# A two-layer decoder trunk on one core: the scheduler orders all queues by its detailed timeline

## The chip, the core and the metric

One core of a Trainium2 chip. The metric is the device time of one execution in microseconds, taken from several runs. The core's engines are TensorE (PE, matrix products), VectorE (DVE), ScalarE (ACT), GpSimd (POOL) and SyncE (SP, which here issues all DMAs). Each has its own queue and works through it in order; semaphores tie the queues together.

## The reference

Two layers over x of 512 tokens by 1024. Each layer normalises and modulates x by a condition vector c, projects it to 3,740 columns, runs four kinds of attention on them (A dilated, B native sparse, C gated linear, D sliding window with sinks), multiplies each by its own gate, projects back, normalises again and adds the result, gated, to x:

```python
shift, scale, gate = jnp.split(jax.nn.silu(c) @ w_ada + b_ada, 3, axis=-1)
h = rms_norm(x, ln_pre) * (1.0 + scale[:, None]) + shift[:, None]
u = split_columns(h @ w_in)
o_a = dilated_attention(a_q, a_k, a_v)
o_b = nsa_attention(b_q, b_kc, b_vc, b_ks, b_vs, b_kw, b_vw, b_g)   # compresses keys and values by w1, w2
o_c = rms_norm(gla_attention(c_q, c_k, c_v, log_a), gla_norm)
o_d = banded_attention(d_q, d_k, d_v, SWA_WIN - 1, sinks)
mixed = jnp.concatenate([o_a * silu(a_z), o_b * silu(b_z), o_c * silu(c_z), o_d * silu(d_z)], axis=-1)
return x + gate[:, None] * rms_norm(mixed @ w_out, ln_post)
```

## The kernel before

All data is float32. Every large product is made of three matmuls on split operands: the operand is cast to a rounded high part (`HH`, `whi`) and the rest is kept as a low part (`HL`, `wlo`); PE adds high·high, high·low and low·high. ACT makes `whi` (L475) and DVE `wlo` (L478).

*Tiles.* x is four row tiles of 128 tokens, `x0` to `x3`. Its normalised, transposed form lies in `HH`/`HL`. Names below carry a serial number (tp_3763), which is that of the tile in the program.

*Start.* `startup` loads x, norms it, transposes (L703), modulates and splits it (`HL` at L711). The modulation is computed by DVE: one L290 reduces a 128x512 slice `wmod` of the modulation weights; 32 of these belong to each layer.

*Projection.* `proj` produces columns transposed (`mm_T`, tile `mmT`, L525, 24 matmuls) or by row tile (`mm_TM`, tile `mmTM`, L536). `load_piece` (L487) loads raw weights into a ring of four buffers, `wraw`; `split_w` puts their halves into a ring of three.

*Attention.* In a layer C comes first (`attn_c`), then B, A and D. C forms the log decay `la` in two DVE steps (L836, L837), sums it on PE (`bp`, L841), gathers the values `vs` by small DMAs (L824) and ends with value products (L953). B multiplies two compression matrices w1, which take slots of the raw-weight ring (`hid`, L1052), transposes the result (`hT`, L1061), and goes on to compressed keys (`kcp`) and scores. In B, A and D a unit is: scores `sc` (L638, L639), maximum `m` (DVE, L755), exponential `p` (ACT, L757), reciprocal and scaling (DVE, L763 to L768), transposes `pT` (L771), copies, value products (L785).

*Beside it.* `merge` calls the attention generators and, between their steps, the projection (`proj`), the first part of the output projection (`out1`, tile `yo`, L1169) and `extras`: in layer 0 the 32 L290 of layer 1, and in both layers the gate, for which DVE sums 16 slices `wada` into `aac` (L348 the first of eight, L350 the rest: "macs" below), PE adds over partitions (L377), DVE adds a row `adab` (L378) and POOL multiplies by `adal` (L380). All slices `wmod`, `wada`, `adab`, `adal` share one ring of two buffers.

*Between the layers.* For each row tile `out2` adds the last part of the output projection (`yo2`, L1169, L1216), then on DVE `y` (L1224), `yg` (L1232) and `xr` (L1237), and norms `y` for the next layer (L438). `turn` transposes it on PE (`tp`, L454, eight matmuls), modulates half by DVE and half by ACT (`hf`, L464, L462), casts `HH` (ACT, L467) and subtracts `HL` (DVE, L468). `mm_TM` then projects the tile's C columns (`mmTM`, 24 matmuls of 332 columns). The program writes these in the order out2 of tile 0, turn 0, out2 of tile 1, turn 1, and so on, then the four products.

*What sets the order.* The source gives each instruction a priority by the place where it is written, shifted here and there by constants. The tile framework's scheduler then simulates the engines in time, takes at each moment for each engine the ready instruction of best priority, and so fixes every queue: PE, DVE, ACT, POOL and SP's DMA issues. Nothing is reordered at run time. The constant `TLS` (line 21) chooses which of two models of time this simulation uses; it is handed over in `make`.

Of the kernel before, what the change touches and what calls it, by code (L numbers as in the profile page):

```python
# [17 lines left out]
EPS = 1e-6  # L18
BIG = 1e30
PRE = 2  # L20
TLS = False
B = dict(raw=4, w=3, mx=3, v4=5, dv=2, ad=2, qk=16, g=8, p=3, sz=4, pt=3, sm=4)
QT = QH = QL = QG = 0
QX = 60
# [1325 lines left out]
def make(arrays):  # L1350
# [3 lines left out]
    out = nc.dram_tensor('out_y', (S, D), F32, kind="ExternalOutput").ap()  # L1354
    with tile.TileContext(nc, schedule_with_timeline_sim=TLS) as tc:
        build(tc, A, out)
# [9 lines left out]
```

## Time and profile before

| | us |
|---|---|
| runs | 694.17, 694.81, 696.92 |
| median | 694.81 |
| the profiled execution | 697.9 |
| its span | 695.7 |

| engine | busy us | share of the span |
|---|---|---|
| PE | 649.8 | 93% |
| PE weight loads | 524.5 | 75% |
| DVE | 498.6 | 72% |
| ACT | 336.8 | 48% |
| POOL | 31.1 | 4% |

The mean granted clock of PE is 0.986 of full speed. HBM moved 125 GB/s over the span. Rows of matmuls are pipelined, and their ends are modelled: a matmul's recorded time is longer than the distance from its start to that of the next. In a table by stretch, length minus busy time of PE is the time in which it did nothing at all. The stretches of the program in the profiled execution are: start 0–52, C of layer 0 52–124, projections and the compression of B 124–174, B, A and D of layer 0 174–313, end of the first output projection 313–348, passage to layer 1 348–384, projections 384–410, C 410–462, projections and compression 462–506, B, A and D 506–657, end of the output 657–696.

### The profile page before, as it was taken

The page shows a single profiled execution, that of the slowest core. Times are in us where ns is not written, and L with a number is a line of the kernel's source. Part 1 is how long each engine was busy: PE and PEld are TensorE (multiplying, and loading weights), DVE is VectorE, ACT ScalarE, POOL GpSimd, SP SyncE. Part 2 cuts the span into 40 slices and gives each one's busy share as a digit, 9 for nine tenths or more (in the row PEclk, how much of TensorE's full clock was granted, in tenths as well). Part 3 has the DMA queues.
Part 4 walks back from the last instruction along what each step waited for, and adds up shares of the span by engine and source line. Part 5 has one row for each costly group of instructions (what it writes and reads, how often), then busy time and mean ns, then how long its engine had stood idle before and what let it go on. Part 6 is the DMA issues. An engine that isn't in the chain of part 4 may idle for free.

```text
span 695.7 us, 11980 instructions
## 1 busy us (share of the span) xinstructions
PE 649.8 (93%) x4460; PEld 524.5 (75%) x4460; DVE 498.6 (72%) x1291; ACT 336.8 (48%) x748; POOL 31.1 (4%) x57
## 2 busy tenths in 40 slices
PE   3999889989998999999998989899999999999996
PEld 1797766877777767779996768678777777778895
DVE  5985889666868787784598467743588878768656
ACT  5454444155565555663475244425545436435432
POOL 2000000000001100000012000000000000000000
PEclk9999999999999999999999999999999999999999
DMA  8955764657204444112642681212520021111143
GB/s 299 391 218 166 256 195 138 185 180 272 77 1 138 136 110 133 34 32 81 207 169 79 180 262 43 63 61 91 165 78 32 17 75 32 46 46 46 48 155 116
DMA packets 38163, 87.89 MB, mean 126 GB/s; under 512 B 4185, under 2 KB 7769, under 8 KB 38106
## 3 DMA queue, kind: packets, MB, share of 16 engines
q1 hardware_dynamic: 38106, 87.14, 38.7%
q8 instruction: 35, 0.57, 0.3%
q14 instruction: 22, 0.18, 0.1%
HBM read 81.88 MB, written 5.24 MB: 125 GB/s over the span
## 4 chain that ended last, share of the span: by engine, by line
PE 58%; DVE 17%; DMA 12%; ACT 6%; issue 4%; POOL 1%; SPq 1%; DVEq 0%; POOLq 0%; ACTq 0%
PE mmT L525 19%; PE yo L1169 9%; PE mmTM L536 5%; PE pT L771 5%; DMA wmod<-in_w_mod 4%; PE ob L785 3%; DMA vs<-vd 3%; DVE wlo L478 2%; DMA wraw<-in_w_in 2%; PE a L719 2%; PE yo L1216 2%; PE sc L638 2%; DVE wmod L290 2%; PE od L1007 2%; PE oa L785 2%
## 5 line engine op out<-in xcount | busy, mean ns | idle before, releaser
L525 PE MATMUL mmT<-HH,whi 128*128 128x512 f32 (+1 forms) x352 | 142.8, 406 | 1.4 <-ACT whi L475 1.4
L525 PE MATMUL mmT<-HH,wlo 128*128 128x512 f32 (+1 forms) x352 | 142.6, 405 | 0.4 <-DVE wlo L478 0.4
L525 PE MATMUL mmT<-HL,whi 128*128 128x512 f32 (+1 forms) x352 | 142.3, 404 | 0.0
L757 ACT ACTIVATE p<-p,m 128x256 f32<-128x256 f32 (+3 forms) x128 | 68.8, 538 | 66.9 <-DVE m L755 62.5
L478 DVE TENSOR_TENSOR wlo<-wraw,whi 128x1024 fp32r<-128x1024 f32 (+3 forms) x60 | 72.2, 1205 | 33.2 <-ACT whi L475 32.9
L475 ACT CAST whi<-wraw 128x1024 fp32r<-128x1024 f32 (+3 forms) x60 | 61.5, 1027 | 56.1 <-PE mmT L525 36.8
L525 PEld LDWEIGHTS mmT<-HH,wlo 128*128 128x128 f32 (+1 forms) x352 | 66.2, 188 | 16.1 <-issue 1.5
L525 PEld LDWEIGHTS mmT<-HH,whi 128*128 128x128 f32 (+1 forms) x352 | 66.4, 189 | 15.3 <-ACT whi L475 1.8
L525 PEld LDWEIGHTS mmT<-HL,whi 128*128 128x128 f32 (+1 forms) x352 | 66.4, 189 | 14.0 <-issue 1.2
L771 PE MATMUL pT<-cst,p 128*128 128x128 f32 x296 | 48.9, 279 | 6.0 <-DVE p L768 2.2
L536 PE MATMUL mmTM<-whi,HH 128*128 128x256 f32 (+1 forms) x160 | 48.6, 304 | 3.2 <-ACT HH L467 2.4
L755 DVE CUSTOM_DVE_ANT_0 p<-sc,cst 128x128 f32<-128x128 f32 (+3 forms) x96 | 44.8, 482 | 7.7 <-PE sc L639 7.3
L771 PEld LDWEIGHTS pT<-cst,p 128*128 128x128 f32 x296 | 33.3, 140 | 22.5 <-issue 11.8
L536 PE MATMUL mmTM<-whi,HL 128*128 128x256 f32 (+1 forms) x160 | 47.4, 297 | 0.4 <-DVE HL L468 0.4
L536 PE MATMUL mmTM<-wlo,HH 128*128 128x256 f32 (+1 forms) x160 | 47.2, 295 | 0.0
L1169 PE MATMUL yo<-wlo,HH 128*128 128x256 f32 x144 | 41.9, 291 | 0.0
L1169 PE MATMUL yo<-whi,HH 128*128 128x256 f32 x144 | 41.7, 290 | 0.0
L1169 PE MATMUL yo<-whi,HL 128*128 128x256 f32 x144 | 41.1, 286 | 0.0
L536 PEld LDWEIGHTS mmTM<-whi,HH 128*128 128x128 f32 x160 | 31.0, 194 | 6.1 <-ACT HH L467 3.5
L638 PE MATMUL sc<-k,x 128*128 128x128 f32 (+3 forms) x96 | 32.7, 352 | 0.5 <-DVE m L755 0.2
L778 DVE COPY pt<-pT 128x256 f32<-128x256 f32 (+3 forms) x60 | 28.4, 498 | 6.4 <-PE pT L771 5.5
L536 PEld LDWEIGHTS mmTM<-whi,HL 128*128 128x128 f32 x160 | 30.9, 194 | 1.9 <-DVE HL L468 0.9
(273 smaller groups left out, 1342.2 us busy)
## 6 DMA issues: line engine op xcount, KB each, us to landing
wraw<-in_w_in SPq DMA_DIRECT2D x52, 512.0 KB, 4.1
wmod<-in_w_mod SPq DMA_DIRECT2D x64, 256.0 KB, 5.4
wada<-in_w_gate SPq DMA_DIRECT2D x32, 256.0 KB, 3.1
wor<-in_w_out SPq DMA_DIRECT2D x12, 512.0 KB, 3.3
w<-in_w SPq DMA_DIRECT2D x8, 512.0 KB, 4.7
vs<-vd SPq DMA_DIRECT2D x24, 128.0 KB, 9.8
x<-in_x SPq DMA_DIRECT2D x8, 256.0 KB, 5.2
wor<-in_w_out SPq DMA_DIRECT2D x8, 256.0 KB, 2.9
```

What stands on the lines that cost most here:

```text
L290: DVE.tensor_tensor_reduce(wt, wt, csr[:, 512 * h:512 * h + 512], 0.5, init, ALU.mult, ALU.add, dst)
L475: ACT.copy(hi, raw)
L478: eng.tensor_tensor(out=lo, in0=raw, in1=hi, op=ALU.subtract)
L525: PE.matmul(acc[:m], a, b, start=(n == 0), stop=(n == 23))
L536: PE.matmul(acc[:, :ncol], a, b, start=(n == 0), stop=(n == 23))
L638: PE.matmul(out, q[e][:, qs], k[e][0][:, ks], start=True, stop=False)
L755: DVE.tensor_tensor_reduce(p[:, c], sc[:, c], mask, -0.125, 1e38 if sink is None else sink[0][:, es[j]:es[j] + 1], ALU.add, ALU.min, m[:, ...
L757: ACT.activation(p[:, c], p[:, c], AF.Exp, bias=m[:, j:j + 1], scale=-1.0, accum_out=lsum[:, j:j + 1])
L771: PE.transpose(tp[:, b:b + 128], p[:, b:b + 128], C('ident'))
L778: DVE.tensor_copy(dst, src)
L785: PE.matmul(o[hs, q0:q1], vt[:, kb, vc:vc + 64], PT[:, 512 * kb:512 * kb + q1 - q0], start=(first and kb == 0), stop=(last and kb == 3), s ...
L1169: PE.matmul(acc[:, :n_], a, b, start=(n == 0), stop=(n == last))
```

## The change

The scheduler's simulation of time uses its detailed timeline in place of its plain one. The source of the computation is untouched: the same instructions, tiles, buffers and priorities, but every queue's order is drawn up anew.

```diff
-TLS = False
+TLS = True
```

Three places, each shown from the queue before and from the queue after.

VectorE between the first modulated piece of row tile 1 and its `HL`, at the passage between the layers; before:

```order
L464 TENSOR_SCALAR hf32_3768<-tp_3763,adags_624,adass_623 128x128
L464 TENSOR_SCALAR hf32_3780<-tp_3775,adags_624,adass_623 128x128
L1232 TENSOR_TENSOR yg_3835<-y2_3181,gl_2188 128x512
L464 TENSOR_SCALAR hf32_3768<-tp_3763,adags_624,adass_623 128x128
L1237 SCALAR_TENSOR_TENSOR xr_3789<-yg_3835,rstd_3839,xr_3789 128x512
L478 TENSOR_TENSOR wlo_3597<-wraw_3594,whi_3596 128x996
L478 TENSOR_TENSOR wlo_3603<-wraw_3600,whi_3602 128x664
L468 TENSOR_TENSOR HL_161<-hf32_3768,HH_160 128x4x128
```

and in the queue after:

```order
L564 TENSOR_TENSOR bg_3994<-mmTM_3967,par_621 128x12
L350 SCALAR_TENSOR_TENSOR aac_4201<-wada_4258,csil_158,aac_4201 128x512
L464 TENSOR_SCALAR hf32_3780<-tp_3775,adags_624,adass_623 128x128
L1232 TENSOR_TENSOR yg_3835<-y2_3181,gl_2188 128x512
L1232 TENSOR_TENSOR yg_3836<-y2_3181,gl_2423 128x512
L464 TENSOR_SCALAR hf32_3768<-tp_3763,adags_624,adass_623 128x128
L350 SCALAR_TENSOR_TENSOR aac_4201<-wada_4339,csil_158,aac_4201 128x512
L464 TENSOR_SCALAR hf32_3780<-tp_3775,adags_624,adass_623 128x128
L1237 SCALAR_TENSOR_TENSOR xr_3789<-yg_3835,rstd_3839,xr_3789 128x512
L1237 SCALAR_TENSOR_TENSOR xr_3789<-yg_3836,rstd_3839,xr_3789 128x512
L468 TENSOR_TENSOR HL_161<-hf32_3768,HH_160 128x4x128
```

Two macs and both steps of tile 2's residual now stand ahead of tile 1's `HL`; the splits of the weights (`wlo`) have gone ahead of tile 0's `HL`, together with two more macs.

TensorE at the transposes of row tile 1 (`tp_3763`, `tp_3775`), same stage; before:

```order
L1216 MATMUL yo2_3890<-wlo_3479,HH_160 128x256
L1216 MATMUL yo2_3890<-whi_3478,HL_161 128x256
L454 MATMUL tp_3763<-cst_105,y1_3180 128x128 x4
L454 MATMUL tp_3775<-cst_105,y1_3180 128x128 x4
L1216 MATMUL yo2_3890<-whi_3478,HH_160 128x256
L1216 MATMUL yo2_3890<-wlo_3479,HH_160 128x256
```

and after:

```order
L536 MATMUL mmTM_3967<-wlo_3603,HH_160 128x332
L536 MATMUL mmTM_3967<-whi_3602,HL_161 128x332
L454 MATMUL tp_3763<-cst_105,y1_3180 128x128 x4
L454 MATMUL tp_3775<-cst_105,y1_3180 128x128 x4
L536 MATMUL mmTM_3998<-whi_3590,HH_160 128x332
L536 MATMUL mmTM_3998<-wlo_3591,HH_160 128x332
```

Before, the rest of tile 3's output product and the product of tile 0 (`mmTM_3967`) stood between the transposes of tile 1 and the product of tile 1 (`mmTM_3998`); after, nothing does. It is the same at tiles 2 and 3.

TensorE behind the compression of layer 1 (`hT_5155` is the transpose that ends it; `mmT_5329` is the first product on weights that load into the slots of w1); before:

```order
L1061 MATMUL hT_5155<-cst_105,hbuf_5152 128x128
L525 MATMUL mmT_5259<-HH_160,whi_5060 128x512
L525 MATMUL mmT_5259<-HL_161,whi_5060 128x512
L525 MATMUL mmT_5259<-HH_160,wlo_5061 128x512
L525 MATMUL mmT_5259<-HH_160,whi_5060 128x512
```

and after:

```order
L525 MATMUL mmT_5259<-HH_160,whi_5060 128x512
L525 MATMUL mmT_5259<-HL_161,whi_5060 128x512
L525 MATMUL mmT_5259<-HH_160,wlo_5061 128x512
L1061 MATMUL hT_5155<-cst_105,hbuf_5152 128x128
L525 MATMUL mmT_5329<-HH_160,whi_5184 128x512
L525 MATMUL mmT_5329<-HL_161,whi_5184 128x512
```

The product `mmT_5259` has moved from behind `hT_5155` to before it.

## Rows read from the trace of the kernel before

**Rows 1.** The page: busy time by engine, and the chain by engine.
```profile
PE 649.8 (93%) x4460; PEld 524.5 (75%) x4460; DVE 498.6 (72%) x1291; ACT 336.8 (48%) x748; POOL 31.1 (4%) x57
...
PE 58%; DVE 17%; DMA 12%; ACT 6%; issue 4%; POOL 1%; SPq 1%; DVEq 0%; POOLq 0%; ACTq 0%
```
**Rows 2.** Busy time by stretch; the heading row names the columns.
```profile
core 0: us, PE busy (x) PEld busy (x) DVE busy (x) ACT busy (x) POOL busy (x), PEclk, DMA share, GB/s
52.00:124.00 72.00, 65.37 (x646) 49.91 (x645) 57.45 (x129) 31.78 (x52) 2.69 (x4) 0.95 0.62 187
...
174.00:313.00 139.00, 133.42 (x781) 101.73 (x780) 111.36 (x345) 81.15 (x229) 5.02 (x6) 1.00 0.28 82
313.00:348.00 35.00, 34.27 (x270) 32.38 (x269) 17.00 (x30) 13.73 (x29) 1.09 (x2) 1.00 0.44 144
348.00:384.00 36.00, 32.58 (x205) 29.59 (x206) 31.03 (x67) 24.11 (x57) 6.65 (x12) 0.95 0.38 124
...
410.00:462.00 52.00, 46.41 (x564) 35.84 (x563) 36.94 (x77) 24.32 (x41) 4.66 (x5) 0.97 0.28 90
...
506.00:657.00 151.00, 149.43 (x893) 115.74 (x892) 120.13 (x382) 72.19 (x190) 2.44 (x4) 1.00 0.15 46
```
**Rows 3.** Waits: engine, line, waited for; us in total, times, longest.
```profile
ACT p L757 <- DVE m L755: 62.5, 37, 6.9
...
PE bp L841 <- DVE la L837: 3.0, 1, 3.0
...
PE ms L972 <- DVE lo L356: 2.1, 1, 2.1
```
**Rows 4.** Busy time in two stretches of 1.5 us (columns as rows 2).
```profile
376.00:377.50 1.50, 0.00 (x0) 0.00 (x0) 0.90 (x4) 1.47 (x5) 0.00 (x0) 1.00 0.47 164
380.50:382.00 1.50, 1.50 (x7) 1.50 (x7) 1.23 (x1) 0.23 (x1) 0.00 (x0) 0.50 0.94 291
```
**Rows 5.** DVE in time: start, busy, line, out<-in, count, [idle before <-releaser].
```profile
352.25 0.69 DVE L468 TENSOR_TENSOR HL<-hf,HH 128x512 fp32r<-128x512 f32 x1
...
357.11 0.72 DVE L464 TENSOR_SCALAR hf<-tp,adags,adass 128x128 f32<-128x128 f32 x2
357.74 0.68 DVE L1232 TENSOR_TENSOR yg<-y,gl 128x512 f32<-128x512 f32 x1
358.34 0.40 DVE L464 TENSOR_SCALAR hf<-tp,adags,adass 128x128 f32<-128x128 f32 x1
358.66 0.74 DVE L1237 SCALAR_TENSOR_TENSOR xr<-yg,rstd,xr 128x512 f32<-128x512 f32 x1
359.32 1.95 DVE L478 TENSOR_TENSOR wlo<-wraw,whi 128x996 fp32r<-128x996 f32 x2
361.19 0.68 DVE L468 TENSOR_TENSOR HL<-hf,HH 128x512 fp32r<-128x512 f32 x1
...
377.55 0.69 DVE L468 TENSOR_TENSOR HL<-hf,HH 128x512 fp32r<-128x512 f32 x1 [0.59 <-ACT HH L467]
```
**Rows 6.** DVE in time: one mac of the gate in layer 0.
```profile
217.18 0.75 DVE L350 SCALAR_TENSOR_TENSOR aac<-wada,csil,aac 128x512 f32<-128x512 f32 x1 [1.62 <-DMA wada<-in_w_gate]
```
**Rows 7.** The chain in time, 340 to 384: start, us, what, count.
```profile
341.23 0.73 PE yo L1169 x6
...
360.08 3.67 PE mmTM L536 x24
```
**Rows 8.** Tile `wmod` in 50–215 (ns min/median/max); SP's gathers in time.
```profile
L290 DVE CUSTOM_DVE_ANT_0 wmod<-wmod,csr,par x16: 737/750/1197, 57.1 to 145.1; 128x512 f32<-128x512 f32 x16
...
DMA to landing us min/median/max: 2.6/2.7/2.8
...
56.08 10.85 SPq L824 DMA_DIRECT2D vs<-vd  x11
```
**Rows 9.** Behind the compression of layer 1: the chain, then ACT in time.
```profile
493.13 6.60 DMA wraw<-in_w_in
...
497.14 1.05 ACT L475 CAST whi<-wraw 128x1024 fp32r<-128x1024 f32 x1 [1.01 <-DMA wraw<-in_w_in]
```

## The prediction

> **What bounds the kernel now.** I read the totals by engine and the chain that ended last first [rows 1]. PE is busy 93% of the span and holds 58% of the chain; DVE, ACT and DMA hold 35% together, so the end is set by PE work strung between short waits for the others. The change moves no work from one engine to another, so only these waits can move.
>
> I then cut the span where the program changes what it does [rows 2]. Length minus PE busy is what PE stood idle: 6.6 us in C of layer 0 (52–124), 5.6 in B, A and D of layer 0 (174–313), 3.4 at the passage between the layers (348–384), 5.6 in C of layer 1 (410–462) and 1.6 in B, A and D of layer 1 (506–657). The rows on waits name the causes: the softmax exponential waits for DVE's maximum 37 times, and PE waits once for the logarithmic decay `la` (3.0 us), once for a half-split operand `lo` (2.1) [rows 3]. A pause costs more than itself. PE did nothing in 376–377.5, and in 380.5–382 the granted clock was 0.50, its lower level [rows 4].
>
> Busy time hides some slack: a product `mmTM` of 24 matmuls passes in 3.67 us, 0.15 each [rows 7], while a record is about twice as long. The Trainium skill, page "Perfetto Trace Analysis", section "Identifying the Most-Contended Engine", says that matmul busy time is a bad measure and weight-load busy time a good one; by that the room is 25% of the span and not 7%. These rows agree that records overlap; I still sum from idle time, since slack inside dense products is not what an order can remove.
>
> **The change, step by step.** Every queue runs in order. The instructions are the same, 3,766 matmuls among them; what differs is who stands before whom. The sum is made against the profiled execution (697.9 us, its span 695.7 and 2.2 around it); the median of the runs is 694.8, and I carry the difference over unchanged.
>
> *Head and C of layer 0: +1.5 us (bounds −4 and +6).* Two halves of layer-1 modulation (L290) come ahead of the last `HL` of the start: 2 × 0.75 = 1.5 [rows 8]. In C, loads of weights stand ahead of the 11 `vs` gathers that occupy SP for 10.85 us [rows 8]; that can take away the wait for the weights behind them. Against it, one L290 now stands between the two steps of `la` (L836, L837), and 12 more L290 and the 8 macs L348/L350 of the first gate half are queued before C's last level: 20 × 0.75 = 15 us of DVE. DVE is idle 72 − 57.5 = 14.5 us there [rows 2], and each needs a load of 2.7 us into a ring of two buffers [rows 8]. That only just fits. The 111 projection matmuls that now precede C's last value product give PE its work meanwhile. I take nought for C and the 1.5; the lower bound is the 6.6 us idle there less what a DVE so full must leave open, the upper one eight loads that each come 0.75 late.
>
> *Compression weights of layer 0: +2.5 (0 to +6).* The two matrices w1 (`hid`) hold slots of the raw-weight ring; the next weights load when `hid` has read them. The nearest row is layer 1: loads issued at 493.1 run 6.6 us, the first cast comes at 497.14 [rows 9]. In layer 0 four matmuls and a transpose remain between `hid` and the product on those weights, where a whole product (24) stood: about 3 us open. The following `kcp` and `pcT` have lost some cover too (I take 1.5), and the wait for `lo` of 2.1 [rows 3] goes. 3 + 1.5 − 2.1 = 2.4.
>
> *Attention of layer 0: −7 (−9 to −2).* Between the scores of a unit and its transposes PE needs other work while DVE and ACT make the softmax. For unit sc_2425 six projection matmuls stood there, now 24 and eight value products; most units show the like. 5.6 us are idle [rows 2], PE's queue now changes from one source line to another 692 times instead of 784, and the slack at such changes adds the rest. This cover is borrowed: 91 matmuls `yo` of 0.12 us [rows 7], 10.9 us, that ran after D's last value product now run before it.
>
> *The passage between the layers: +14 (+9 to +20).* Here the borrowed cover is missed. PE now does the second output products of all four row tiles first, and the transposes of tiles 1 to 3 stand directly before the product that needs them. What PE then waits for is DVE, whose first `HL` of tile 0 starts at 352.25 and that of tile 3 at 377.55 before, 8.4 us a tile [rows 5]: DVE was the bound already (31.0 of 36 us [rows 2]), and PE's output products hid it. By rows [rows 5, 6], four `hf` take 1.3, two `yg` 1.2, two `xr` 1.3, one `HL` 0.6 from start to start, two `wlo` 1.9, one mac 0.75. In the new order:
> tile 0: 1.3 + 1.2 + 1.3 + 1.9 + two macs 1.5 + 0.4 for small ones + `HL` 0.6 = 8.2, beside 30 matmuls of 0.12 = 3.6 [rows 7]: 4.6 open;
> tile 1: 1.3 + 1.2 + 1.3 + two macs 1.5 + 0.3 small + 0.6 = 6.2, beside nothing;
> tile 2: 1.3 + 1.2 + 1.3 + 0.6 = 4.4, since `yg` stands behind a copy out of the product before;
> tile 3: 2.0, as in the kernel before, where PE did nothing in 376–377.5 [rows 4].
> Together 17.2, against 3.4: +13.8. The macs stood behind the passage before, where PE did not need DVE; a load late for one has a row with a wait of 1.62 [rows 6]. The clock is not in this: four pauses of 2 us or more instead of one, and a product at the lower level takes up to twice its 3.67, so the upper end is 20. The lower, 9, holds if PE comes to the passage later than I think and DVE is further ahead.
>
> *C of layer 1: −5.5 (−7 to −2).* No gate macs are left in it, the weights load ahead of the gathers, and the product before `bp` covers the 3.0 us wait [rows 3]. Of 5.6 idle I keep nothing but what the first level needs, and add the clock that this pause took.
>
> *Compression weights of layer 1: +4.5 (+2 to +7).* Here a whole product of 24 stood between `hid` and the product on the new weights; now one transpose does. From issue at 493.1, when `hid` has read them, to the end of the first cast at 497.14 + 1.05 [rows 9] are 5.1; less some 0.6 for the transpose and because the first matrix may be released before the second.
>
> *Attention of layer 1: −2.5 (−4 to +1).* As in layer 0, but only 1.6 us are idle [rows 2]. The tail is as before.
>
> Sum: 1.5 + 2.5 − 7 + 14 − 5.5 + 4.5 − 2.5 = **+7.5**: profiled 705.4, median 694.8 + 7.5 = **702**.
>
> **Rivals.** (1) *The gain stays.* In 313–348 DVE is busy half the time [rows 2], so it might run ahead and meet PE in the passage; then that term is nought and the sum −6.5: 688. Against it: the transposes stand in PE's own queue behind the products, so DVE has nothing to run ahead on. It decides from the point where the first `HL` of tile 1 ends within 2 us of tile 0's product. The Trainium skill, "Perfetto Trace Analysis", section "Optimization Strategy", says that interleaving regimes with different limits may improve a kernel; by it, more projection work inside attention is a gain, and this rival is what it would give. The passage shows the other half: work put into one regime is missing from the next.
> (2) *A wash.* Attention and C give their high ends, −8.5 and −6.5, the passage its low one, 9: near 694.
> (3) *Slower still, in C of layer 0.* If a modulation load lands after DVE reaches it, decays and levels queue behind it: the 15 us of DVE no longer fit in 14.5, and the excess is paid by PE, some 8 more: 710.
>
> **How the numbers follow.** Forecast 0.55; rival 1 0.17; rival 2 0.20; rival 3 0.08. About 0.5% (3.5 us) is what a measurement of this kernel can tell from no change. So slower 0.63, same 0.20, faster 0.17. Range 689 to 713: the low end takes in rival 2 and touches rival 1, the upper one is the clock's share in the passage and rival 3.
>
> **What would show it.** Right: PE idle over 12 us in the passage, in four pauses each ended by `HL` or `HH`, with granted clock 0.5 after them; PE idle under 2 us in B, A, D of layer 0; `mmT` after `hid` of layer 1 waiting some 4 us for `whi`; no 3 us wait at `bp` of layer 1. Wrong: the passage no longer than before, or D of layer 0 ending later for reasons that lie in C.

## The result, and the profile after

| | before | after |
|---|---|---|
| median of the runs, us | 695.21 (694.17 to 696.92, 4 runs) | 745.49 (742.92 to 747.28, 4 runs) |
| span of the profiled execution, us | 695.7 | 745.5 |
| mean granted clock | 0.986 | 0.956 |

The ratio is 1.072 (95% interval 1.068 to 1.076): slower by 50 us, where +7.5 had been forecast. The first and the fourth part of the page of after, which answer [rows 1]:

```profile
PE 663.4 (89%) x4460; PEld 540.8 (73%) x4460; DVE 498.1 (67%) x1291; ACT 334.7 (45%) x748; POOL 30.9 (4%) x57
...
PE 64%; DVE 17%; DMA 9%; issue 4%; ACT 4%; POOL 1%; SPq 1%; DVEq 0%; POOLq 0%; ACTq 0%
```

The counts are the same (4,460 matmuls on either page; the 3,766 of the prediction is on neither) and so is the work of DVE and ACT. PE was idle for 82.1 us of its span instead of 45.9, and its busy time grew by 13.6 us; together that is the 49.8 us by which the span grew. By the mean granted clock some 66 us ran at the lower level (0.5) instead of some 19, which is why the same matmuls were busy for longer. The stretches of after that answer [rows 2], in its columns (C of layer 0; attention of layer 0; the passage; C of layer 1; compression and attention of layer 1):

```profile
52.00:142.00 90.00, 75.65 (x624) 61.29 (x624) 64.09 (x153) 34.32 (x60) 2.69 (x4) 0.91 0.56 173
192.00:336.00 144.00, 132.89 (x759) 103.40 (x760) 109.17 (x335) 78.64 (x224) 5.86 (x6) 0.96 0.24 76
374.00:422.00 48.00, 31.86 (x175) 29.66 (x174) 32.97 (x71) 22.52 (x56) 6.87 (x11) 0.80 0.41 129
448.00:500.00 52.00, 48.36 (x469) 40.03 (x468) 34.49 (x68) 24.48 (x41) 4.34 (x7) 0.97 0.22 72
550.00:706.00 156.00, 147.10 (x890) 116.72 (x889) 120.09 (x383) 71.79 (x191) 2.44 (x4) 0.98 0.14 42
```

Length minus PE busy was 14.4, 11.1, 16.1, 3.6 and 8.9 us. Only the fourth fell. The waits of PE in after (in total, times, longest), to be held against [rows 3]:

```profile
PE mmTM L536 <- ACT HH L467: 11.9, 4, 4.1
...
PE bp L841 <- DVE la L837: 6.6, 1, 6.6
PE mmT L525 <- DVE kl L631: 4.4, 3, 2.1
...
PE mmTM L536 <- DVE HL L468: 4.2, 4, 2.9
PE mmT L525 <- DVE x L621: 4.0, 3, 2.6
PE ada L377 <- DVE aac L350: 3.6, 1, 3.6
```

`HH` and `HL` are the passage, as forecast. `la` is C of layer 0 (not layer 1, where the 3.0 of before went), `aac` is the gate's chain of macs in the attention of layer 0, and `kl` and `x` are products that wait until DVE has emptied a PSUM tile.

Stretches of two kernels don't hold the same work, so I also compare at **equal TensorE work**: each matmul is given the time that its kind usually takes, the times are summed in the order in which a kernel runs them, and for each sum the kernels' clocks are compared. The numbers are us behind before when PE has done so much work. This scale is not that of the span: 140 lies near 138 us of before's span, 340 near 315, 400 near 380 and 600 near 560 (estimates from the traces), so the last column lies ahead of the end, where after is 49.8 us behind by its span. Where a kernel has the old order, such numbers still wander: between 60 and 340, in runs whose order was old up to there, from +1.1 to −5.3. A difference of 3 us in one place of one run therefore says little.

| PE work done, us | 60 | 140 | 180 | 340 | 380 | 400 | 440 | 500 | 600 |
|---|---|---|---|---|---|---|---|---|---|
| after | +1.2 | +13.5 | +13.4 | +23.3 | +19.1 | +40.7 | +37.0 | +38.2 | +50.9 |
| new order, old side steps | +0.7 | −2.6 | +4.1 | +14.7 | +15.8 | +25.1 | +34.4 | +35.5 | +49.7 |
| old order, new side steps | +1.3 | +20.2 | +16.2 | +28.7 | +33.0 | +47.8 | +50.4 | +51.2 | +50.5 |

By this, after lost 12 us in C of layer 0 (60 to 140), 10 in the attention of layer 0 (180 to 340), 17 around the passage (340 to 400), won 2.5 in C of layer 1 (400 to 500), and lost 13 in compression and the first part of the attention of layer 1 (500 to 600).

### The profile page after: what moved, and what is told of

Its sections match the earlier page's. It is cut to its first block, busy times and chain, and to the rows that moved or that the text cites. A ratio compares the mean times of both kernels' runs of the same rounds, so it can differ in the third digit from the quotient of the medians.

```text
span 745.5 us, 11999 instructions
## 1 busy us (share of the span) xinstructions
PE 663.4 (89%) x4460; PEld 540.8 (73%) x4460; DVE 498.1 (67%) x1291; ACT 334.7 (45%) x748; POOL 30.9 (4%) x57
## 4 chain that ended last, share of the span: by engine, by line
PE 64%; DVE 17%; DMA 9%; issue 4%; ACT 4%; POOL 1%; SPq 1%; DVEq 0%; POOLq 0%; ACTq 0%
PE mmT L525 27%; PE yo L1169 9%; PE mmTM L536 7%; DMA wada<-in_w_gate 4%; PE pT L771 3%; PE ob L785 3%; DVE wmod L290 2%; DMA wmod<-in_w_mod 2%; PE yo L1216 2%; DVE wlo L478 2%; PE sc L638 2%; PE sc L639 2%; PE oa L785 2%; DMA vs<-vd 1%; DVE aac L350 1%
## 5 line engine op out<-in xcount | busy, mean ns | idle before, releaser
L525 PE MATMUL mmT<-HH,whi 128*128 128x512 f32 (+1 forms) x352 | 143.9, 409 | 13.5 <-DVE kl L631 4.4
L525 PEld LDWEIGHTS mmT<-HH,wlo 128*128 128x128 f32 (+1 forms) x352 | 67.3, 191 | 17.4 <-DVE wlo L478 2.3
L536 PE MATMUL mmTM<-whi,HH 128*128 128x256 f32 (+1 forms) x160 | 53.1, 332 | 15.7 <-ACT HH L467 11.9
L536 PE MATMUL mmTM<-whi,HL 128*128 128x256 f32 (+1 forms) x160 | 52.1, 326 | 4.2 <-DVE HL L468 4.2
L536 PE MATMUL mmTM<-wlo,HH 128*128 128x256 f32 (+1 forms) x160 | 51.7, 323 | 0.0
L771 PE MATMUL pT<-cst,p 128*128 128x128 f32 x296 | 47.4, 278 | 2.0 <-DVE p L768 0.9
L536 PEld LDWEIGHTS mmTM<-whi,HH 128*128 128x128 f32 x160 | 35.3, 221 | 18.9 <-ACT HH L467 12.8
L771 PEld LDWEIGHTS pT<-cst,p 128*128 128x128 f32 x296 | 35.1, 141 | 13.4 <-issue 7.0
L536 PEld LDWEIGHTS mmTM<-whi,HL 128*128 128x128 f32 x160 | 35.0, 219 | 5.7 <-DVE HL L468 5.5
```

The source lines that it names most:

```text
L525: PE.matmul(acc[:m], a, b, start=(n == 0), stop=(n == 23))
L536: PE.matmul(acc[:, :ncol], a, b, start=(n == 0), stop=(n == 23))
L771: PE.transpose(tp[:, b:b + 128], p[:, b:b + 128], C('ident'))
```

## The experiments

In all of them the scheduler is off duty: behind the program's build, every queue is chained in a recorded order, which fixes who stands before whom. The chain itself costs nothing that can be seen: old_warm and the two mend kernels below are chained in (nearly) the old order and run at before's time.

```diff
         build(tc, A, out)
+        pin(tc, nc)
```

What differs between the kernels is the recorded order; it is given as a diff in words or in queue rows. "Old" is the order of before, "new" that of after.

### Side steps against the rest, and the stages one by one

*Side steps* are the L290 of layer 1, the macs of the gate and what belongs to them (loads, sums, `adab`, `adal`, products of L377).

**new_extras_old**

```diff
-order: new
+order: new, the side steps at their old places
```

> The new order (745 us), but the layer-1 modulation and the gate (L290 of layer 1, L348, L350, their loads, L377, L378, L380) stand where the old order has them. Theory 1, that these side steps are what PE's pauses hang on: VectorE was held 8.6 us by a modulation load in C of layer 0 and 3.6 us at the gate sum in attention, and six macs stand in the passage between the layers; with the clock that each pause took this is 11 + 6 + 6 us, so about 722. Theory 2, that the order of TensorE's own queue (products pulled ahead of attention, transposes directly before their products) is the cause: about 740.

Measured: 743.7 us, 1.070 (1.058 to 1.083), near theory 2. The table above shows where: the loss in C of layer 0 is gone and the passage costs 9 instead of 22 us (380 to 400), but the same end is reached, 9 us of it in C of layer 1. There a mac now stands on DVE in front of `ca`, from which the decay is made, and its load was issued on SP behind ten gathers (at 424.87) and took 8.8 us to land:

```profile
433.73 0.75 DVE L350 SCALAR_TENSOR_TENSOR aac<-wada,csil,aac 128x512 f32<-128x512 f32 x1 [12.13 <-DMA wada<-in_w_gate]
```

```profile
PE zp L830 <- DVE ca L591: 9.3, 1, 9.3
```

**old_extras_new**

```diff
-order: old
+order: old, the side steps placed as in the new order
```

> The old order (695 us), with only the same side steps placed as the new order has them. Theory 1: the loss comes along, 710 to 718. Theory 2: within 3 us of 695.

Measured: 747.2 us, 1.075 (1.069 to 1.081), far above both theories. Moving the side steps alone, in an otherwise old order, costs as much as the whole change: 19 us in C of layer 0, 12 in the attention of layer 0, 19 around the passage. So the side steps are enough for a loss of this size, and by the run before they are not needed for it: the two do not add up. Both orders are whole. A mixture can lose at its seams what neither order loses (old_att1_pe_new and old_att1_dve_new below show it), so such a run alone doesn't say what a part costs in the whole new order.

**new_till_C0, old_passage_new, old_C1_new, old_att1_new**, one stage new and the rest old:

```diff
-order: old
+new_till_C0: new up to the last value product of C of layer 0, then old
+old_passage_new: old, from the end of D of layer 0 to the last mmTM new, then old
+old_C1_new: old, from the last mmTM to the end of C of layer 1 new, then old
+old_att1_new: old, from the end of C of layer 1 to the end of D new, then old
```

> The new order up to the last value product of C in layer 0 (124 us before, 136 after), the old one for all that is left. If what C of layer 0 lost (11 us) is lost for good: about 706. If it is lead that later stages give back: under 700.

> The old order, except that from the last value product of D in layer 0 to the last of the four first products of layer 1 it is the new one. If the passage is slow by its own order: 21 us lost between 380 and 400 us of work in the new order, so about 714. If it is slow because attention had used up the cover before it: under 705.

> The old order up to the last first product of layer 1, then the new one up to the last value product of C in layer 1, then the old one. In the new order this stretch gained 3.7 us; if the gain is the stage's own, 690 to 693; if it came from gate macs that had already run, 695 or more, since here VectorE still has six of them to do.

> The old order up to the last value product of C in layer 1, then the new one up to the last value product of D in layer 1, then the old one. No modulation runs here and no passage. In the new order 12 to 14 us were lost between 440 and 600 us of work. If TensorE's queue itself loses them (the compression weights reached without cover, products waiting for PSUM that VectorE has not emptied): 695 + 12, 705 to 710. If they come from what was late before this stage: within 3 us of 695.

Measured: 702.9 (1.011, 1.006 to 1.017), 712.9 (1.026, 1.020 to 1.031), 702.8 (1.011, 1.002 to 1.019) and 707.2 us (1.017, 1.008 to 1.026). At equal work each stage costs something alone: C of layer 0 9.9 us at its end (7.7 by the kernel's time); the passage 22.6 (17.7 by time); the attention of layer 1 12.5 (12.3). With the 14.0 of the attention of layer 0 (old_att0_new_macs_old below) the four times add up to 52 us, about the whole loss; the seams make this no proof. C of layer 1 alone shows no gain: it loses 12.7 us ahead of itself (400 to 420), where seven macs stand in a row on DVE (380 to 391 us), each behind its own load, and PE waits 9.7 us for the `wlo` behind them; it wins back 2.5 by 500. So what after wins there, it seems to win because these macs have already run in the passage.

### How much of it is the clock

After ran at the lower clock (0.5) in 13 stretches of 3.4 to 6.9 us, before in five of 3.4 (the end apart). Idle products on constants, placed on PE where it waits, are meant to keep the clock up and change no other queue.

```diff
+        def warm(key, acc):
...
+            for _ in range(_WARM.get((key, n), 0)):
+                _EXTRA.append(PE.matmul(acc[:, :128], C('triu'), C('triu'), start=True, stop=True))
```

old_warm has 31 of them in four pauses of the old order, new_warm 65 in the passage of the new one.

> The old order with 31 idle matmuls of 128x128 on constants, put into four of TensorE's pauses ahead of the matmul that waits, into the PSUM tile that it overwrites: 5 before mmT_881, 8 before att0_1029, 11 before bp_4289, 7 before mmTM_4054. They take nothing from the result. If each pause of 2 us or more costs a stretch at half clock behind it (1.7 us each, four of the five such stretches), about 688; if the clock falls for another reason, or the idle matmuls delay what waits, 695 to 698.

> The new order with 65 such idle matmuls in the passage between the layers: 20 before mmTM_3967, 21 before mmTM_3998, 14 before mmTM_4026, 10 before mmTM_4054. In the new order the clock was low there for 20 us in all, 10 us of work lost. If the pauses bring the clock down and the low clock lengthens the passage: 735 to 738. If VectorE sets the pace of the passage anyway: 743 to 746.

Measured: old_warm 694.9 against 694.9 us (0.9994, 0.996 to 1.003), new_warm 742.3 (1.067, 1.060 to 1.075). The passage of new_warm (the stretch that had 0.80 in after):

```profile
374.00:422.00 48.00, 42.56 (x291) 40.18 (x290) 32.44 (x67) 22.69 (x54) 4.77 (x9) 0.93 0.39 126
```

In the old order the medians agree. The eight runs of old_warm had a mean clock of 0.992 to 0.997 (median 0.996), the nine of before beside it 0.984 to 0.994 (median 0.991), so there were 0.5% of clock to win, 3.5 us if all of it were time, and by the interval no more than some 3 came. The profiled executions show more, since that of before is one of its slower runs: all five low stretches are gone, 17 us at half speed, and the span is 3.5 us shorter (692.2 against 695.7). Among the runs of before time and clock go together: the fastest, 690.8 us, had 0.998, and the three slowest, over 698.5, had 0.984 to 0.989. That does not tell which of the two brings the other. In the passage of new_warm PE is at 0.93 and busy for 42.6 us, the 65 idle products among them, and the passage is 1.1 us shorter at equal work: there DVE sets the pace, and products at half speed fill time in which PE would have waited. Outside the passage no run raised the clock of the new order. Some 41 us of its low stretches lie there, against 14 in before; at half speed that difference is 14 us of work (an estimate), of which old_warm lets one expect a part. How much of the loss in C of layer 0 and in the attention it makes is not shown.

### The passage: its turns or the macs

**old_passage_new_macs_old**

```diff
-order: old_passage_new
+order: old_passage_new, the side steps at their old places
```

> The order of before, with the passage between the layers as the new order has it, but the side steps (the gate's modulation: loads, scaling, adding, its products) at their old places. With the side steps at the new places the same passage cost 22.6 us at equal TensorE work and the whole kernel 712.9 us against 695.2. Theory (the macs that stand among the turns' steps on VectorE are about half of the passage's loss): +9 to +12 us in the passage, 702 to 705 us. Rival (the order of the turns on TensorE and VectorE alone makes the loss, the macs fill holes): +20 or more in the passage, 711 to 714 us. Second rival (the macs are all of it): within 2 us of 695.

Measured: 711.3 us (1.022, 1.018 to 1.026), only 1.6 less than with the macs. At equal work it lost 9.9 us between 380 and 400, as the theory said, but another 4 on the way there (340 to 380), where the macs' place had won 2.2. The waits in the passage, first of old_passage_new, then of this run:

```profile
PE mmTM L536 <- ACT HH L467: 13.0, 4, 5.4
PE mmTM L536 <- DVE HL L468: 4.2, 4, 2.9
```

```profile
PE mmTM L536 <- ACT HH L467: 10.0, 4, 3.2
PE mmTM L536 <- DVE HL L468: 1.6, 4, 0.6
```

11.6 us instead of 17.2 (16.1 in after): by the kernel's time the order of the turns is most of the loss, as the rival said. The macs make the pauses 5.6 us longer, but taking them out brought only 1.6 us, so at their old places they cost elsewhere what they cost here.

### C of layer 0: the load behind the gathers

In after the two steps of `la` and what stood between them on DVE (start, us, [idle before <- what ended it]):

```profile
66.70 0.69 DVE L836 TENSOR_SCALAR la<-zp 128x512 f32<-128x512 f32 x1
76.01 0.75 DVE L290 CUSTOM_DVE_ANT_0 wmod<-wmod,csr,par 128x512 f32<-128x512 f32 x1 [8.62 <-DMA wmod<-in_w_mod]
...
76.69 0.69 DVE L837 TENSOR_TENSOR la<-la,t 128x512 f32<-128x512 f32 x1
```

and SP's queue at that time:

```profile
59.93 10.14 SPq L824 DMA_DIRECT2D vs<-vd x10
70.90 2.03 SPq L282 DMA_DIRECT2D wmod<-in_w_mod x2
```

The load of that L290 was issued behind ten gathers. DVE stood still for 8.6 us in front of `la`, and PE waited 6.6 us at `bp`.

**C0_load_early** moves two loads on SP and nothing else:

```diff
 SP L817 v<-vd x2
+SP L282 wmod<-in_w_mod x2
 SP L824 vs<-vd x10
-SP L282 wmod<-in_w_mod x2
```

> As new_till_C0 (the new order until the last value product of C of layer 0, then the old one; 702.9 us, 9.9 us behind at equal TensorE work at the end of C), with one thing put back: two modulation loads stand on SP's queue ahead of the last ten vs gathers instead of behind them. Nothing moves on TensorE, VectorE, ScalarE or GpSimd. Theory (VectorE stands 8.2 us at the mac of L290 only because its load is issued behind 10 us of gathers): the wait of VectorE there falls from 8.2 us to under 1, and the kernel gains 6 to 8 us on new_till_C0 at the end of C: 695 to 698 us. Rival (the load would be late for other reasons, its two-buffer ring or the transfers themselves, or TensorE waits next for the gathered vs): 700 to 703 us.

Measured: 702.2 us (1.011, 1.006 to 1.015), the rival's number, but not for the rival's reasons. The wait in front of `la` did go: the L290 started at 66.89, and PE had no wait at `bp`; at 80 us of work the kernel was level with before (+0.1; new_till_C0 +8.6). At 100 it was +7.9. DVE in that kernel, some 14 us later:

```profile
80.70 0.75 DVE L290 CUSTOM_DVE_ANT_0 wmod<-wmod,csr,par 128x512 f32<-128x512 f32 x1 [5.06 <-DMA wmod<-in_w_mod]
...
81.38 0.42 DVE L858 TENSOR_TENSOR u<-u 128x256 f32<-128x256 f32 x1
```

and PE:

```profile
81.85 1.01 PE L860 MATMUL dp<-cst,u 128*128 128x4 f32 x4 [4.19 <-DVE u L858]
```

The next pair of L290 stands in front of the next step that PE needs, and its loads were issued behind the gathers and three weight loads (74.82). So the mechanism is load-fed steps queued ahead of the decay's chain, with loads issued behind gathers, and putting one right hands the wait to the next. All of them out of the stage is new_extras_old, in which it ran 2.6 us ahead; there the same thing came in C of layer 1 (the 12.13 us above).

### Attention of layer 0

The forecast was that pauses in front of `pT` would go. They did. PE's waits in this stage of before (174 to 313, the first three of six) and of after (192 to 336, without the 3.6 us for `aac` above):

```profile
PE pT L771 <- ACT p L757: 1.8, 2, 1.4
PE pT L771 <- DVE p L768: 1.4, 4, 0.5
PE pT L771 <- DVE l L763: 1.1, 2, 0.6
```

```profile
PE mmT L525 <- DVE kl L631: 2.1, 1, 2.1
PE sc L638 <- DVE m L755: 2.0, 2, 1.8
PE sc L638 <- DVE smc L1108: 1.2, 1, 1.2
PE mmTM L536 <- DVE x L621: 1.0, 1, 1.0
```

Of 5.6 us idle in before 4.6 were at `pT`; of 11.1 in after 0.8 are, and the others are new. The longest is the chain of macs (start, us, what; between 230 and 249):

```profile
232.05 2.69 DMA wada<-in_w_gate
234.77 0.98 DVE aac L350
...
239.59 2.71 DMA wada<-in_w_gate
242.33 0.77 DVE aac L350
243.11 2.60 DMA wada<-in_w_gate
245.80 0.75 DVE aac L350
...
247.88 1.12 PE ada L377 x2
```

Load and mac follow each other through the ring of two buffers, and PE waits 3.6 us for the sum. Is this the stage's loss, or the other waits?

**old_att0_new_macs_old**

```diff
-order: old
+order: old, from the end of C to the end of D of layer 0 new, side steps at their old places
```

> The order of before, with the attention of layer 0 as the new order has it, but the side steps (macs of the gate, their loads and products) at their old places. Theory (as in layer 1, the new order of this stage loses by itself, in pauses of 1 to 2 us in front of products whose operand or PSUM tile VectorE gives late; the macs add to it): +6 to +14 us inside 130 to 310 us, 701 to 709 us. Rival (all of this stage's loss in the new order was its load-and-mac chain): within 2 us of 695, or a gain of 2 to 9 us as forecast from the pauses that the old order has there.

Measured: 710.0 us (1.021, 1.015 to 1.026), 14 us more than before and just above the theory, so the stage loses in its own order and not only by the macs' new places. One wait of 5.4 us at the same product is among it, since the chain of macs ends too late for PE here as well (its old place in a new order is a seam); the rest is pauses of up to 1.7 us.

### Attention of layer 1

PE's waits in 480 to 660 of old_att1_new, then the stretch (columns as above):

```profile
PE mmT L525 <- ACT whi L475: 1.7, 1, 1.7
PE mmT L525 <- DVE kl L631: 1.4, 1, 1.4
PE sc L638 <- DVE smc L1108: 1.2, 1, 1.2
```

```profile
480.00:660.00 180.00, 167.34 (x992) 131.15 (x992) 127.87 (x398) 83.30 (x206) 2.71 (x6) 0.98 0.17 56
```

and the same stretch of before:

```profile
480.00:660.00 180.00, 177.81 (x1079) 139.20 (x1078) 135.58 (x413) 88.97 (x216) 2.70 (x6) 1.00 0.19 59
```

12.7 us idle instead of 2.2, in many small pauses. Whose order is it?

**old_att1_pe_new, old_att1_dve_new**

```diff
-order: old
+old_att1_pe_new: old, PE's queue of the stage as in old_att1_new as far as the others allow
+old_att1_dve_new: old, DVE's queue of the stage as in old_att1_new as far as PE's allows
```

> The order of before, with TensorE's queue alone in the attention of layer 1 as near to the new order as VectorE's and ScalarE's old queues allow (VectorE's is moved in 15 instructions, ScalarE's in 2). All queues new there cost 12.5 us (707.2 us). Theory (TensorE's new order asks for operands and empty PSUM tiles in another order than the old queues of VectorE and ScalarE give them, so the products' order is the cause): 706 to 715 us, all of it inside 430 to 620 us of the span. Rival (the order of VectorE and ScalarE is the cause, TensorE's order is harmless): 694 to 698 us.

> The order of before, with VectorE's queue alone in the attention of layer 1 as near to the new order as TensorE's old one allows (VectorE moved in 160 instructions of the 181 that differ, which shifts 204 of TensorE's in turn). Theory (TensorE's new order is the cause): at most +5 us, 695 to 700 us. Rival (VectorE's new order is the cause): +9 to +14 us, 704 to 709 us, in pauses of TensorE in front of products whose operand VectorE or ScalarE gives.

Measured: 785.9 (1.129, 1.125 to 1.133) and 803.5 us (1.154, 1.150 to 1.159). Both theories failed by 70 us and more. Waits of PE in the second, 480 to 730:

```profile
PE pT L771 <- DVE pt L778: 22.8, 16, 3.9
PE sc L638 <- DVE m L755: 13.7, 11, 3.9
PE pT L771 <- DVE p L766: 13.2, 5, 3.8
```

Now the softmax chain is late in unit after unit. An order is a matter of all queues together: the loss can't be put down to one engine's queue by exchanging it.

**old_att1_new_mended** takes the pauses as the trace names them and moves five DVE steps out of the way:

```diff
 DVE L1107 smc
-DVE L478 wlo
 DVE L1108 smc
 DVE L1107 smc
 DVE L620, L621 x
 DVE L1108 smc
+DVE L478 wlo
...
+DVE L630, L631 kl
 DVE L801 mx
 DVE L768 p
 DVE L763 l
 DVE L778 pt x2
-DVE L630, L631 kl
```

and two more `wlo`, one behind five scalings of `p` and one behind an `x`.

> As old_att1_new (the old order, the attention of layer 1 new: 707.2 us, 12.5 us lost there), with five of VectorE's 1291 instructions moved a few places each: a wlo behind the mask step and the x that TensorE waits for, two kl ahead of four steps, a wlo behind an x, and a wlo behind five scalings of p. Nothing else moves. Theory (the loss is single VectorE steps, 0.4 to 1.2 us each, queued in front of the one that TensorE waits for): the pauses of 1.2 + 1.0, 1.5, 1.0 and 1.1 + 0.9 us at these places go or halve, 4 to 6 us come back: 701 to 703.5 us. Rival (these pauses only show that VectorE is late as a whole; the next step is late in their place): 706 to 708 us.

Measured: 707.2 us (1.017, 1.012 to 1.021), nothing gained, as the rival said; the waits for `smc` and `kl` went, and among those that came is

```profile
PE pT L771 <- DVE l L763: 2.0, 1, 2.0
```

**old_att1_new_pool, old_pool**: nine of the stage's `wlo` on GpSimd, in the new and in the old order.

```diff
-            eng = eng or (POOL if nsplit[0] % WLO_MOD in WLO_POOL else DVE)
+            eng = POOL if nsplit[0] in [60, 61, 62, 63, 64, 65, 66, 67, 68] else (eng or (POOL if nsplit[0] % WLO_MOD in WLO_POOL else DVE))
```

> As old_att1_new (old order, the attention of layer 1 new; 707.2 us), with nine subtractions wlo of the weights in that stage made by GpSimd instead of VectorE, at the same places in the order. VectorE loses 9 x 1.2 = 11 us of its work there. GpSimd is idle there; by its 1.73 us for 128x512 one wlo takes some 3.5 us. Theory (VectorE as a whole is late in the new order of this stage, so that moving five of its steps only moved the pauses): half or more of the 12.5 us comes back, 698 to 702 us. Rival (it is not VectorE's amount of work but the order in which TensorE asks, and the same steps stay late): 705 to 709 us. Second rival (the longer wlo is itself what TensorE then waits for): over 709 us, with waits of mmT for wlo.

> The order of before with the same nine wlo on GpSimd, to tell what the engine change is worth by itself. Both theories: TensorE is idle for 1.6 us in that stage in before, so no more than 1 us can be gained: 694 to 696.5 us; if the longer wlo is waited for, more.

Measured: old_att1_new_pool 703.6 us (703.35 to 707.33; 1.015, 1.010 to 1.019), old_pool 696.5 (1.003, 1.000 to 1.005). 703.6 lies between the theories; the profiled execution is the slow end of the three, and in it the stage at equal work lost 11.8 us, as with `wlo` on DVE. By the medians the loss against before falls from 12.3 to 8.9 us, or to 7.1 against old_pool; the intervals leave 3 to 6 us either way. So with 11 us of work off DVE more than half of the loss stays: DVE's load as a whole is at most a part of the cause. What the rest is, stays open.

### A version faster than both

**mend_C0_C1** and **mend_C0_C1_ahead**: C of layer 0 from new_extras_old (it was 2.6 us ahead there), the rest old; in C of layer 1 the decay is moved forward, in the first kernel past a cast, a mac and a `wlo`, in the second (the diff) further: the three `t` ahead of the cast, the first `la` ahead of two macs, the second ahead of a `wlo`. The two macs still stand between the steps of `la`.

```diff
+ACT L833, L834, L835 t
 ACT L475 whi
-ACT L833, L834 t
 ACT L475 whi
-ACT L835 t
...
+DVE L836 la
 DVE L350 aac x2
+DVE L837 la
 DVE L478 wlo
-DVE L836 la
 DVE L610 x
 DVE L350 aac
 DVE L478 wlo
-DVE L837 la
```

> A candidate for a version faster than both. The head and C of layer 0 in the new order but with the side steps at their old places (in the whole new order with old side steps that stage ran 3.9 us ahead of before at 120 us of TensorE work and 2.6 ahead at 140, and gave it back in the attention that followed), then the old order; and in C of layer 1 the last two steps of the decay (the third t on ScalarE, the second la on VectorE) ahead of a cast, a mac and a wlo that stood in front of them (TensorE waits 3.0 us there in before; the table load of 1.28 us that now starts earlier leaves a gain of 1 to 2 us). Theory (both gains hold when the stages behind keep their old order): 690 to 692.5 us against 695, ratio 0.993 to 0.997. Rival (the old order's stages behind C of layer 0 rest on what C's order had already done, and give the gain back): 693.5 to 697 us.

> A second candidate for a version faster than both. Head and C of layer 0 as in mend_C0_C1 (which held 2.4 to 3.0 us there until C of layer 1 and lost 5 us in C of layer 1, where the decay steps stood behind a weight cast that waits for its load: TensorE stood 4.6 us in front of bp). Now the three t on ScalarE stand ahead of that cast, the first la step ahead of the two macs and the second ahead of the first wlo: nothing in the decay stands behind a load. Theory: the pause of 3.0 us (4.6 in mend_C0_C1) in front of bp goes, TensorE is 5 to 7 us ahead of before at 420 us of the span: 688 to 690.5 us against 695, ratio 0.990 to 0.994. Rival (the cast and the macs, now behind the decay, are what TensorE then waits for): 692 to 696 us.

Measured: 696.9 against 695.4 us (1.002, 1.000 to 1.004) and 695.8 against 696.0 (0.999, 0.997 to 1.002). In the first, `bp` waited 4.4 us, longer than before: the three t stood on ACT behind a cast that waits for its load.

```profile
405.73 1.05 ACT L475 CAST whi<-wraw 128x1024 fp32r<-128x1024 f32 x1 [8.35 <-DMA wraw<-in_w_in]
```

In the second the wait at `bp`, 3.0 us in [rows 3], is gone, and PE stands instead at the products behind it:

```profile
409.92 1.06 PE L841 MATMUL bp<-cst,la 128*128 128x128 f32 x8
411.44 1.10 PE L377 MATMUL ada<-aac,ones 128*128 128x512 f32 x2 [0.47 <-DVE aac L350]
414.37 1.06 PE L850 MATMUL dp<-cst,qkd 128*128 128x4 f32 x8 [1.83 <-DVE qkd L847]
```

At equal work 0.5 us were won there. Both times fell in the rival's range; no version beat before.

## Why the prediction was wrong

The side was right, the size was not: +7.5 forecast, +50 measured, outside the range. That the side came right is in part luck: of the 50 us only the passage's 17 had been forecast as a loss of that size, and the attention of layer 0, which lost 10, as a gain of 7. Term by term, with the measured values from the first row of the table:

| term | forecast | measured |
|---|---|---|
| head and C of layer 0 (to 140) | +1.5 | +13.5 |
| compression weights of layer 0 (140 to 180) | +2.5 | −0.1 |
| attention of layer 0 (180 to 340) | −7 | +9.9 |
| passage (340 to 400) | +14 | +17.4 |
| C of layer 1 and projections behind it (400 to 500) | −5.5 | −2.5 |
| compression weights and attention of layer 1 (500 to 600) | +4.5 − 2.5 | +12.7 |

*C of layer 0: the step that failed is "that only just fits".* It compared 15 us of DVE work with 14.5 us of room and gave each load its own 2.7 us. The room was never the limit: in after DVE was busy for 64.1 of the stage's 90 us. It did not ask when the loads are issued. The loads stand on SP behind 10.1 us of gathers, which I had listed in the same paragraph for another purpose, and DVE waited 8.6 us for one of them between the two steps of `la`. Rival 3 had this mechanism (a load that lands after DVE reaches it, the decay behind it), at a chance of 0.08 and a price of 8, though it gave full queues and not the gathers as its reason; C0_load_early shows its place, and that it acts more than once.

*Attention of layer 0: the step that failed is the cover.* I took more PE work between a unit's scores and its transposes for a gain, and counted the pauses of the old order as what could be won. (The 62.5 us of [rows 3] that I named as a cause are waits of ACT; PE's own at `pT` are the 4.6 us above.) The cover did grow. By the two orders, PE work between the scores and the transposes of a unit is, at the median of a layer's units, 5.2 us before and 9.3 after in layer 0, and 5.9 and 8.1 in layer 1. The waits at `pT` fell with it. Yet both stages lost. Cover on PE's queue says that PE comes late enough for the softmax; it says nothing of where on DVE's queue the steps stand that other products need. In place of the pauses at `pT` there are now those of `mmT` for `kl`, `sc` for `m` and `smc`, `mmTM` for `x`. That this happens is read from the waits; that old_att0_new_macs_old and old_att1_new lose 14 (5.4 of it at the macs' product) and 12 us with the stages around them in the old order shows that it is the stages' own order. Why those steps are late was tried in three ways in layer 1 (one queue exchanged, five steps moved, nine steps taken off DVE) and is not settled. The gate's chain of macs, 3.6 us here, was no term of the sum at all.

*Passage: right in kind and nearly in size.* The pauses that I summed per tile as 4.6, 6.2, 4.4 and 2.0, together 17.2, are in after 4.7, 5.0, 3.8 and 2.7, together 16.1 (`HH` and `HL` of a tile together; the waits for `HL` are 2.90, 0.84, 0.33 and 0.16). The first product of each tile:

```profile
383.30 0.42 PE L536 MATMUL mmTM<-whi,HH 128*128 128x332 f32 x1 [1.84 <-ACT HH L467]
...
397.97 0.65 PE L536 MATMUL mmTM<-whi,HH 128*128 128x332 f32 x1 [4.14 <-ACT HH L467]
...
408.99 0.42 PE L536 MATMUL mmTM<-whi,HH 128*128 128x332 f32 x1 [3.43 <-ACT HH L467]
...
418.26 0.42 PE L536 MATMUL mmTM<-whi,HH 128*128 128x332 f32 x1 [2.49 <-ACT HH L467]
```

The reason is shown as far as it goes by old_passage_new and old_passage_new_macs_old: with the turns' order alone 13.8 us are lost between 340 and 400. That this is the forecast's number is in part luck, for 3 us of the forecast were macs. What came on top is for the most part not the clock, which I had allowed for in the upper end: new_warm raised it in the passage from 0.80 to 0.93 and 1.1 us came back. The rule of the Trainium skill, "TensorE: Matmul & The Clock Gate", section "Terms", that the penalty is the throttled time less its granted share, would make the gain of new_warm's profiled execution over that of after 13.6 us (32.8 at a mean clock of 0.956 less 19.2 at 0.974, an estimate). This trace does not bear it out: the two spans differ by 5.8 us, and the medians of the runs by 3.2.

*C of layer 1: mis-sized.* No wait at `bp` of layer 1 is left in after, and PE idled 3.6 us instead of 5.6. I had assumed that a pause of 3 us is worth 3 us and its low clock besides; 2.5 us came, within the bounds. mend_C0_C1_ahead removed exactly this pause and won 0.5: products behind it waited in its place, 2.3 us together.

*Compression weights of layer 1: right in kind.* PE waits for the cast of the weights, 1.8 us in after and 1.7 in old_att1_new, where 4.5 were forecast and 2 was the lower bound. In layer 0 nothing was lost.

*Rivals.* The gain did not stay, and there was no wash: there was no gain to stay. The chance of slower, 0.63, was on the right side; the range was too narrow because the bounds of three terms (C of layer 0 up to +6, the attention of layer 0 up to −2, that of layer 1 up to +1) ended far below what came. Of the four signs of being right, two came: the four pauses of the passage, and no wait at `bp` of layer 1. The attention of layer 0 idled 11.1 us, not under 2, and the wait for `whi` was 1.8 us, not 4. A term that says "this stage has more cover now" had no reason that excluded a loss.

## What to carry to other kernels

A queue that is drawn up anew by another model of time is a new kernel: cost each stage on all queues, and give a stage's term a bound on the side of loss unless a row excludes it. Before a load-fed step is let in front of a step that another engine waits for, look at when its load is issued and what stands in front of it on the issuing queue, not at its own duration. In this case DVE stood 8.6, 5.1 and 12.1 us for loads that were issued behind gathers. A pause that is named in the trace is worth its length only if nothing else is late behind it; here three mends (C0_load_early, old_att1_new_mended, mend_C0_C1_ahead) each removed the wait they aimed at, and none won time that could be measured.

## What the runs showed of the hardware

Raising the mean granted clock from 0.991 to 0.996 (medians of nine and of eight runs) by 31 idle products changed nothing in the old order that can be measured (0.9994, 0.996 to 1.003). Ten gathers of 128 KB held SP's queue for 10.1 us, and with two loads moved ahead of them the wait of DVE for the first went from 8.2 us (new_till_C0) to nothing. And `wlo` of 128x1024 took 2.38 us on GpSimd, the mean of nine, where I had expected 3.5 from its 1.73 us for half the size in another operation; on DVE it takes 1.2.
